# First FFN of a two-layer block: four groups of four and one of six, residual tiles in free space, early first products, weight sums issued one by one

## The chip, the cores and the metric

One core of a Trainium2 chip runs the whole program in one launch. The metric is device microseconds; the time given is the median of the runs, and the kernel before takes 1605.9 us.

## The reference

Two layers work on 512 image tokens and 256 context tokens of 1024 features in float32. Layer 0 mixes by Fourier and long convolution, layer 1 by attention, and each ends in a gated FFN with a three-tap convolution along the tokens. The change lies in the first FFN:

```python
def _conv_ffn(h, w_up, conv_w, conv_b, w_down):        # D_MODEL 1024, D_FF 2816
    gate, val = jnp.split(h @ w_up, 2, axis=-1)
    return (jax.nn.silu(_dwconv3(gate, conv_w, conv_b)) * val) @ w_down

x = x + g2 * _conv_ffn(_modulate(_rms_norm(x, norm2[i]), sh2, sc2), *ffn)
ctx = ctx + cg2 * _conv_ffn(_modulate(_rms_norm(ctx, norm2[i]), csh2, csc2), *ffn)
```

The six shifts, scales and gates of each layer come from `silu(c) @ w_mod + b_mod`; part of that matrix-vector product for layer 1 is done during this FFN.

## The kernel before

Both token sets lie side by side in rows of 772 columns: 512 tokens, two zeros, 256 context tokens, two zeros. Features lie on the 128 partitions, so an activation is eight tiles. A float32 operand is split into a high part (ScalarE, `hi`, L214) and a low rest (VectorE, `lo`, L219), and each product is three matmuls, high by high, high by low and low by high (`mm3`, L239 to L241). A weight is loaded on SyncE's queue (SP) into a `wr` buffer (L227), of which there are three, and split into a `wh` and a `wl` buffer, three each.

The hidden width 2816 is 22 blocks of 128, called f. Blocks 0 and 1 are plain products. For blocks 2 to 21 each 2x2 product of half weights by half activations is done with seven products instead of eight, P1 to P7 (12 matmuls each, 386 columns), from sums of activation quarters (T1 to T4, with halves Th and Tl) and sums of weight quarters (`suma`, `sumb`). A weight sum starts in S1: on GpSimd's queue (POOL) both sums are first filled by a copy, then the second quarter is added by two accumulating transfers. VectorE adds the third quarter in S2 and S4. Ha, La, Hb and Lb split the sums; Rv, Hv, Lv and Rg, Hg, Lg load and split the value and gate quarters.

The elementwise steps of a block: K1, C1 to C4, Ua, Ub and Xv combine the seven products out of PSUM into `fv` and `fg`; Ca, Cb and Cc are the convolution, Si the silu, Ml the product, Ah and Al the split of the result into `acts`.

`UP0_GROUPS` (L164) collects blocks into six groups. For all but the last, Rd, Hd and Ld load and split the blocks of `w_dn`, D multiplies them for each of the eight output tiles m, X scales the result into one of two `delta` tiles (ScalarE, two instructions), and Y adds it to the residual `xs` in DRAM (POOL, accumulating transfer, L1586). For the last group Rk, Hk and Lk prepare all eight weights in tiles of their own (`keep`), the FFN's pools are given up, the residual is loaded from `xs` into tiles `xr` (L1298), and `res_proj` does the closing products: first the 512 image columns for every m, then the 260 others, each added by VectorE to `xr` (L1232). Behind each m the norm of layer 1 takes its sum of squares (L344, L351, L357), scales (L390) and splits.

Rm loads a row block of `wmodT` into a `wr` buffer, 56 in all, and G does one product with it on VectorE (L320, L321), 80 in all: two for each of the first 24 blocks, one for each later one. `self.sb` holds the two vectors for these products.

The order of all these steps is written out in `UP0_ORDER` (L124). Within a `manual_schedule` block every engine executes its own steps in that order, SP and POOL their transfers too; an engine that waits holds back what is behind it. Tiles of a pool wait for the last user of the same memory (`reuse_waits="tile"`). In this stage PSUM has six tiles of 512 columns (`mm`) and two more (`ms`); before the closing products the pool is opened anew with three of 1024.

Of the kernel before, what the change touches and what calls it, by code (L numbers as in the profile page):

```python
# [18 lines left out]
P = 128  # L19
# [105 lines left out]
S1.2 Rv2 Rm0 Rm1 S2.2 T1 G0 U1a T3 Ca0 Hv2 Cb0 Th3 T2 Ha2 Cc0 Th2 T4 Si0 Tl3 Th1.3 U1b Th1.0 Ml0 Th1.1 Th1.2 Tl1.3 Ah0 Tl2 Al0 Lv2 G1 Tl1.0 Tl1.1 Tl1.2  # L125
P1.2 La2 Th4 G2 P2.2 K1.2 Tl4 P5.2 S4.2 Ca1 C1.2 Rv3 G3 Hb2 P6.2 Cb1 Rg2 Rm2 Lb2 Cc1 P7.2 S1.3 Hv3 Ua2 Si1 Lv3 Hg2 Ml1 P1.3 Lg2 Ah1 Xv2 G4 P4.2 K1.3
Al1 Ub2 G5 C2.2 S2.3 P3.2 C4.2 Ha3 S4.3 Ca2 Rv4 La3 P2.3 Hb3 C3.2 Rg3 Cb2 P5.3 Rm3 Lb3 Cc2 S1.4 Hv4 P6.3 C1.3 Si2 Lv4 Hg3 Ml2 P7.3 Lg3 Ah2 Ua3 G6 P1.4
Al2 Xv3 P4.3 G7 K1.4 Ub3 S2.4 C2.3 Ha4 S4.4 P3.3 C4.3 Rm4 La4 Ca3 P2.4 Cb3 Rv5 Hb4 C3.3 Cc3 Rg4 P5.4 Lb4 Si3 G8 S1.5 P6.4 Hv5 Ml3 Hg4 C1.4 Ah3 Lv5 P7.4
Al3 Lg4 P1.5 Ua4 G9 Xv4 P4.4 Rm5 K1.5 Ub4 S2.5 C2.4 Ha5 S4.5 P3.4 C4.4 Rd0.0 La5 Ca4 Rg5 G10 P2.5 Hb5 C3.4 Cb4 P5.5 Hd0.0 G11 Hg5 Cc4 Rm6 P6.5 Lb5 Si4
C1.5 S1.6 Ml4 P7.5 Ld0.0 Ah4 Lg5 Rm7 Al4 D0.0 Ua5 Rd0.1 G12 Xv5 G13 P4.5 Ub5 Rv6 G14 Hd0.1 C2.5 G15 P3.5 Ld0.1 X0.0 Rm8 C4.5 D0.1 S2.6 Ca5 Y0.0 C3.5  # L130
Rd0.2 S4.6 Hv6 Cb5 Ha6 Lv6 Cc5 Rg6 P1.6 X0.1 La6 Si5 G16 Y0.1 P2.6 Hb6 Ml5 K1.6 Hg6 Lb6 Ah5 P5.6 C1.6 Hd0.2 S1.7 Al5 Ld0.2 P6.6 Lg6 G17 P7.6 Ua6 Rd0.3
Xv6 Rm9 D0.2 Ub6 Rd0.4 C2.6 Hd0.3 Ld0.3 G18 Rd0.5 P4.6 X0.2 G19 Y0.2 P3.6 Rv7 C4.6 Ca6 D0.3 Cb6 Hd0.4 Hd0.5 C3.6 Ld0.4 Cc6 Rm10 Ld0.5 Si6 S2.7 Rm11
D0.4 Ml6 X0.3 S4.7 Hv7 Y0.3 G20 Lv7 D0.5 X0.4 G21 Rd0.6 Ha7 Y0.4 G22 Rg7 La7 P1.7 G23 X0.5 Hb7 Rm12 Y0.5 P2.7 Hg7 Lb7 K1.7 Lg7 S1.8 P5.7 Hd0.6 C1.7
Ld0.6 G24 Rd0.7 P6.7 Rv8 G25 P7.7 Rm13 Ua7 Xv7 Hd0.7 D0.6 Ld0.7 Ub7 Rd1.0 C2.7 S2.8 G26 S4.8 P4.7 G27 X0.6 Y0.6 P3.7 C4.7 Ca7 D0.7 Cb7 Hv8 C3.7 Ha8 Cc7
Lv8 Si7 La8 Rg8 P1.8 Rm14 Ah6 Ml7 X0.7 Al6 P2.8 Ah7 Y0.7 K1.8 Al7 Hb8 P5.8 Hg8 G28 Hd1.0 Lb8 P6.8 C1.8 S1.9 Ld1.0 Lg8 Rd1.1 P7.8 G29 Rd1.2 Ua8 Rm15
D1.0 Xv8 Ub8 C2.8 Hd1.1 Ld1.1 Rd1.3 G30 P4.8 X1.0 G31 Y1.0 P3.8 C4.8 Ca8 D1.1 Cb8 Hd1.2 Hd1.3 C3.8 Ld1.2 Cc8 Rd1.4 Ld1.3 Rv9 Si8 Ml8 D1.2 X1.1 Rm16 Ah8
# [24 lines left out]
C2.21 P4.21 X4.3 Y4.3 P3.21 C4.21 Ca21 D4.4 Cb21 Hd4.5 Hd4.6 Ld4.5 C3.21 Rk0 Cc21 Ld4.6 Si21 D4.5 Rk1 X4.4 Ml21 Hd4.7 Y4.4 Ld4.7 Hk0 Rk2 D4.6 Lk0 X4.5
Rk3 Hk1 Y4.5 Lk1 Rk4 D4.7 Hk2 X4.6 Lk2 Rk5 Hk3 Y4.6 Lk3 Ah21 Rk6 X4.7 Al21 Hk4 Y4.7 Lk4 Hk5 Lk5 Rk7 Hk6 Lk6 Hk7 Lk7
"""
UP0_GROUPS = ((0, 4), (4, 8), (8, 12), (12, 15), (15, 18), (18, 22))  # L164


class Builder:
# [94 lines left out]
    def setup(self):  # L262
# [17 lines left out]
        self.sb = self.t(self.sbp, [P, 2, D], F32, "sb")  # L280
# [32 lines left out]
    def gemv_dve(self, i, jt, conds=(0, 1), raw=None):  # L313

        nc = self.nc
        raw = raw or self.wraw(self.I["wmodT"][i, jt])
        for j in conds:
            junk = self.t(self.sbp, [P, D], BF16, "junk", 1)
            acc = self.t(self.sm, [P, 1], F32, "gacc", 4)
            nc.vector.scalar_tensor_tensor(junk, raw, 1.0, self.sb[:, j, :], op0=ALU.mult, op1=ALU.mult, accum_out=acc)  # L320
            nc.vector.tensor_tensor(self.mod[i][:, jt, j : j + 1], acc, self.col(f"bm_{i}", jt), op=ALU.add)  # L321
# [195 lines left out]
    def mixer(self):  # L517
# [26 lines left out]
        with self.tc.manual_schedule(engines={ENG.PE, ENG.DVE, ENG.SP, ENG.Activation}):  # L544
# [102 lines left out]
            for j in range(2):  # L647
                nc.sync.dma_start(self.sb[:, j, :], I["cboth"][j : j + 1, :].partition_broadcast(P))
# [588 lines left out]
    def layer0(self):  # L1237
# [50 lines left out]
        acts, keep = self.ffn_first(hh, hl, u, xs, first, rest.steps, gl1)  # L1288
# [1330 lines left out]
```

## Time and profile before

| | |
|---|---|
| median of 3 runs | 1605.9 us (1604.74 to 1613.03) |
| profiled execution | 1603.81 us, span 1602.0 us |
| TensorE busy | 1534.1 us (96%) |
| VectorE, ScalarE, GpSimd busy | 1304.3, 770.1, 272.9 us |
| read and written in HBM | 200.47 and 24.74 MB |

Times are from one profiled execution, in us from the start of its span. A wait is given with the instruction that ended it. Matmuls overlap: a 386-column matmul is shown as lasting 0.34 us and the next one starts 0.18 us after it, so a product's time is read from starts. "Granted clock" is the share of TensorE's full clock in a stretch.

### The profile page before, as it was taken

The numbers are of one execution on the slowest core, as the hardware profiler recorded it, in microseconds if no ns is written. First come the engines' busy times: TensorE is split into PE (matmuls) and PEld (weight loads), VectorE is DVE, ScalarE is ACT, GpSimd is POOL, SyncE is SP. The second block draws the span as 40 slices with busy tenths as digits, with TensorE's granted clock in tenths as the row PEclk, the third lists the DMA queues.
The fourth block names the chain that finished last, engine by engine and source line by source line (L and its number), as shares of the span: only waits on it lengthen the run. The fifth ranks groups of instructions, "written<-read, shape, count | busy, mean of one in ns | idle before, by whom it ended". The sixth has DMA issues, their size and how long they took to land.

```text
span 1602.0 us, 23289 instructions
## 1 busy us (share of the span) xinstructions
PE 1534.1 (96%) x8728; PEld 1321.0 (82%) x8728; DVE 1304.3 (81%) x2212; ACT 770.1 (48%) x1177; POOL 272.9 (17%) x421
## 2 busy tenths in 40 slices
PE   7999998999899999999899889999999899999998
PEld 5787888888899999999889777666549799999997
DVE  6788869978998769878677576899996899878884
ACT  4451224436444334434344335989874654435442
POOL 0022125201011211212121000222130022112100
PEclk9999998999999999999999999999999999999999
DMA  9336512545368796898974810000025366565543
GB/s 353 115 114 212 170 40 80 191 138 179 94 158 194 182 215 158 211 245 221 245 184 92 279 40 20 7 18 14 1 56 195 92 163 164 152 155 147 147 115 105
DMA packets 87822, 226.73 MB, mean 142 GB/s; under 512 B 10651, under 2 KB 20061, under 8 KB 86685
## 3 DMA queue, kind: packets, MB, share of 16 engines
q1 hardware_dynamic: 62365, 161.18, 30.4%
q0 software_dynamic: 25344, 64.08, 19.7%
q8 instruction: 68, 1.11, 0.3%
q14 instruction: 45, 0.37, 0.1%
HBM read 200.47 MB, written 24.74 MB: 141 GB/s over the span
## 4 chain that ended last, share of the span: by engine, by line
PE 41%; DVE 17%; DMA 8%; issue 3%; ACT 2%; POOL 1%; SPq 0%; DVEq 0%; ACTq 0%; POOLq 0%
PE mm L239 9%; PE mm L241 9%; PE mm L240 9%; DMA wr<-wmodT 4%; DVE junk L320 3%; DVE wl L219 2%; PE pv L1999 2%; PE ms L239 2%; PE ms L240 2%; PE ms L241 2%; DVE S L1975 1%; DMA wr<-w_up 1%; DMA suma<-w_up 1%; PE s L1945 1%; DVE wr L2014 1%
## 5 line engine op out<-in xcount | busy, mean ns | idle before, releaser
L214 ACT ACTIVATE wh<-wr 128x1024 fp32r<-128x1024 f32 (+4 forms) x185 | 157.4, 860 | 234.6 <-PE mm L240 128.4
L239 PE MATMUL mm<-hh,wh 128*128 128x256 f32 (+3 forms) x696 | 231.9, 333 | 4.6 <-ACT wh L214 1.8
L241 PE MATMUL mm<-hh,wl 128*128 128x256 f32 (+3 forms) x696 | 229.2, 329 | 5.9 <-DVE wl L219 5.9
L240 PE MATMUL mm<-hl,wh 128*128 128x256 f32 (+3 forms) x696 | 230.3, 331 | 2.5 <-DVE hl L397 2.3
L219 DVE TENSOR_TENSOR wl<-wr,wh 128x1024 fp32r<-128x1024 f32 (+4 forms) x185 | 182.7, 993 | 27.6 <-ACT wh L214 27.4
L320 DVE SCALAR_TENSOR_TENSOR junk<-wr,sb 128x1024 bf16<-128x1024 f32 x128 | 156.1, 1219 | 22.9 <-DMA wr<-wmodT 22.7
L239 PEld LDWEIGHTS mm<-hh,wh 128*128 128x128 f32 x696 | 133.4, 192 | 17.4 <-ACT wh L214 2.3
L241 PEld LDWEIGHTS mm<-hh,wl 128*128 128x128 f32 x696 | 132.8, 191 | 16.8 <-DVE wl L219 8.6
L240 PEld LDWEIGHTS mm<-hl,wh 128*128 128x128 f32 x696 | 133.2, 191 | 13.2 <-DVE hl L397 3.3
L1999 PE MATMUL pv<-S,V 128*128 128x512 f32 x192 | 93.8, 597 | 2.5 <-ACT S L1978 2.5
L239 PE MATMUL ms<-hh,wh 128*128 128x386 f32 (+2 forms) x240 | 76.7, 319 | 1.9 <-DVE fg L1474 1.2
L241 PE MATMUL ms<-hh,wl 128*128 128x386 f32 (+2 forms) x240 | 76.4, 318 | 1.8 <-DVE wl L219 1.8
L240 PE MATMUL ms<-hl,wh 128*128 128x386 f32 (+2 forms) x240 | 76.2, 318 | 0.0
L1971 POOL PARTITION_ALL_REDUCE mx<-mx x16 | 45.3, 2834 | 163.4 <-DVE mx L1968 163.4
L239 PE MATMUL mm<-ah,wh 128*128 128x512 f32 x176 | 69.6, 396 | 0.0
L240 PE MATMUL mm<-al,wh 128*128 128x512 f32 x176 | 69.6, 396 | 0.0
L241 PE MATMUL mm<-ah,wl 128*128 128x512 f32 x176 | 69.6, 395 | 0.0
L1586 POOL DMA_DIRECT2D xs<-delta x40 | 34.1, 853 | 203.8 <-ACT delta L216 201.3
L1953 ACT ACTIVATE S<-s,rks 128x512 f32<-128x512 f32 x96 | 62.9, 686 | 12.2 <-PE pv L1999 8.3
L239 PE MATMUL mm<-x,wh 128*128 128x512 f32 x192 | 65.3, 340 | 0.0
L240 PE MATMUL mm<-x,wh 128*128 128x512 f32 x192 | 65.2, 339 | 0.0
L241 PE MATMUL mm<-x,wl 128*128 128x512 f32 x192 | 65.0, 338 | 0.0
(503 smaller groups left out, 4521.3 us busy)
## 6 DMA issues: line engine op xcount, KB each, us to landing
wr<-wmodT SPq DMA_DIRECT2D x80, 512.0 KB, 4.6
wr<-w_up SPq DMA_DIRECT2D x48, 512.0 KB, 4.3
sum<-w_up POOLq DMA_DIRECT2D x80, 256.0 KB, 4.3
xs<-delta POOLq DMA_DIRECT2D x40, 386.0 KB, 6.2
wr<-w_dn SPq DMA_DIRECT2D x48, 256.0 KB, 4.1
suma<-w_up POOLq DMA_DIRECT2D x40, 256.0 KB, 5.0
sumb<-w_up POOLq DMA_DIRECT2D x40, 256.0 KB, 5.2
wr<-w_up SPq DMA_DIRECT2D x40, 256.0 KB, 3.5
```

What stands on the lines that cost most here:

```text
L214: self.nc.scalar.activation(dst, src, AF.Copy)
L219: (eng or self.nc.vector).tensor_tensor(dst, src, hi.bitcast(F32), op=ALU.subtract)
L239: mmul(out, wh, xh, start=start, stop=False)
L240: mmul(out, wh, xl, start=False, stop=False)
L241: mmul(out, wl, xh, start=False, stop=stop)
L320: nc.vector.scalar_tensor_tensor(junk, raw, 1.0, self.sb[:, j, :], op0=ALU.mult, op1=ALU.mult, accum_out=acc)
L1586: nc.gpsimd.dma_start(xs[m], k_["x", g, m], accum_op=ALU.add)
L1945: nc.tensor.matmul(ps, k_[0], q[0], start=True, stop=True)
L1953: nc.scalar.activation(c.S[a][j // 3][:, j % 3, :], c.ps[a, j], AF.Copy, scale=c.r[:, g : g + 1])
L1971: nc.gpsimd.partition_all_reduce(c.m[a][:, 1, :], c.m[a][:, 0, :], P, bass.bass_isa.ReduceOp.max)
L1975: v.tensor_tensor(c.S[a][h], c.S[a][h], mb.to_broadcast([P, 3, T]), op=ALU.subtract)
L1999: nc.tensor.matmul(c.P[a], V[:, j, o : o + 128], c.S[a][j // 3][:, j % 3, :], start=j == 0, stop=j == 5)
```

## The change

- The groups are (0, 4), (4, 8), (8, 12), (12, 16) and (16, 22), five instead of six; a D step of the fourth group has four blocks, the closing products have six.
- S1 becomes two steps, Sa and Sb, each a copy and its accumulating transfer on POOL, with a place of its own in the order.
- The two vectors in `sb` become two tiles. From row block 24 on only the first is read, and Rm loads into the place of the second instead of a `wr` buffer.
- `acts` of the slots 4 and 5 move into a pool `hfa` that stays open until attention. The residual tiles are taken from the top down, so that 7, 6 and 5 lie over the FFN's tiles and the first ones in free space.
- Weights 0 and 1 of the closing products are split into the common `wh` and `wl` buffers, 2 to 5 into `keep`, 6 and 7 during the closing products; weight 0 is loaded and split once more for the second pass, whose order is 1, 6, 7, 2, 3, 0, 4, 5.
- Ea does the first five of six blocks of output tiles 0 and 1 (512 columns) before the last block is ready. PSUM keeps its six tiles of 512 columns until the closing products are done.
- `UP0_ORDER` is another order throughout. Its beginning, a later piece and its end are shown.

```diff
 UP0_ORDER = """
-S1.2 Rv2 Rm0 Rm1 S2.2 T1 G0 U1a T3 Ca0 Hv2 Cb0 Th3 T2 Ha2 Cc0 Th2 T4 Si0 Tl3 Th1.3 U1b Th1.0 Ml0 Th1.1 Th1.2 Tl1.3 Ah0 Tl2 Al0 Lv2 G1 Tl1.0 Tl1.1 Tl1.2
-P1.2 La2 Th4 G2 P2.2 K1.2 Tl4 P5.2 S4.2 Ca1 C1.2 Rv3 G3 Hb2 P6.2 Cb1 Rg2 Rm2 Lb2 Cc1 P7.2 S1.3 Hv3 Ua2 Si1 Lv3 Hg2 Ml1 P1.3 Lg2 Ah1 Xv2 G4 P4.2 K1.3
...
-C2.21 P4.21 X4.3 Y4.3 P3.21 C4.21 Ca21 D4.4 Cb21 Hd4.5 Hd4.6 Ld4.5 C3.21 Rk0 Cc21 Ld4.6 Si21 D4.5 Rk1 X4.4 Ml21 Hd4.7 Y4.4 Ld4.7 Hk0 Rk2 D4.6 Lk0 X4.5
-Rk3 Hk1 Y4.5 Lk1 Rk4 D4.7 Hk2 X4.6 Lk2 Rk5 Hk3 Y4.6 Lk3 Ah21 Rk6 X4.7 Al21 Hk4 Y4.7 Lk4 Hk5 Lk5 Rk7 Hk6 Lk6 Hk7 Lk7
+Sa2 Rv2 Sb2 Rv3 Rg2 S2.2 T1 S4.2 T3 U1a Ca0 Hv2 T2 Th3 Cb0 Th2 T4 Ha2 Cc0 Hg2 Tl3 Si0 Th1.3 U1b Ml0 Th1.0 Th1.1 Th1.2 Tl1.3 Ah0 Tl2 Al0 Lv2 Tl1.0 Rm0
+Tl1.1 Tl1.2 La2 Lg2 Sa3 P1.2 Th4 Hb2 P2.2 Tl4 K1.2 Lb2 P5.2 Ca1 C1.2 Hv3 Sb3 Cb1 P6.2 Lv3 Cc1 P7.2 Ua2 Si1 G0 P1.3 Ml1 Xv2 Ah1 S2.3 P4.2 Ub2 K1.3 Al1
...
+P5.16 Si15 Hd3.0 C1.16 Sb17 G64 P6.16 Ml15 Rm41 Ld3.0 Ah15 P7.16 Hv17 Ua16 Rd3.1 Al15 Rg17 Xv16 D3.0 Lv17 Ub16 G65 C2.16 Rm42 S2.17 P4.16 X3.0 S4.17
...
+Lv21 D3.7 Ub20 S2.21 G78 C2.20 Rm55 S4.21 P4.20 Ah18 Rk1 Ah19 Al18 X3.7 P3.20 Al19 Hg21 C4.20 Y3.7 Lg21 Ca20 P1.21 G79 Rk2 Ha21 C3.20 Hb21 Cb20 P2.21
+K1.21 La21 Cc20 P5.21 Hk0 Lb21 Si20 C1.21 P6.21 Ml20 Lk0 Ah20 Rk3 P7.21 Al20 Hk1 Ua21 Lk1 P4.21 Xv21 Rk4 Ub21 C2.21 P3.21 C4.21 Ca21 Ea0 Cb21 Hk2 C3.21
+Hk3 Cc21 Hk4 Lk2 Si21 Lk3 Rk5 Ea1 Ml21 Lk4 Ah21 Al21 Hk5 Lk5
 """
-UP0_GROUPS = ((0, 4), (4, 8), (8, 12), (12, 15), (15, 18), (18, 22))
+UP0_GROUPS = ((0, 4), (4, 8), (8, 12), (12, 16), (16, 22))
...
-        self.sb = self.t(self.sbp, [P, 2, D], F32, "sb")
+        self.sb = [self.t(self.sbp, [P, D], F32, f"sb{j}", 1) for j in range(2)]
...
         self.close("hf2")
-        self.close("psA")
-        self.ps = self.pool("psA", space=PSUM)
-        self.mmw = 1024
         self.zero_pads(hh[:4] + hl[:4])
         self.xp = self.pool("xres")
+        x = [self.t(self.xp, [P, TW], F32, f"xr{d}") for d in reversed(range(KD))][::-1]
         nt = self.pool("nt", bufs=5)
-        x = [self.t(self.xp, [P, TW], F32, f"xr{d}") for d in range(KD)]
         for d in range(KD):
             nc.sync.dma_start(x[d], xs[d])
...
+        def product(m, c, n, first=0, ps=None):
+            ps = ps or self.mm()
+            for k in range(first, nk):
+                w = slice(128 * k, 128 * k + 128)
+                self.mm3(ps[:, 0:n], keep[m][0][:, w], keep[m][1][:, w], acts[k][0][:, c : c + n], acts[k][1][:, c : c + n], k == 0, k == nk - 1)
+            return ps
...
+        for m in range(KD):
+            if keep[m] is None:
+                keep[m] = self.wload(I["w_dn2"][0, m], 128 * nk)
+            add(m, product(m, 0, T, nk - 1, eps[m]) if m in eps else product(m, 0, T), 0, 0, T, 0)
+            ahook(0, m, m)
+        for j, m in enumerate((1, 6, 7, 2, 3, 0, 4, 5)):
+            add(m, product(m, T, 260), T, C0, C0 + C, 1)
+            if j == 0:
+                keep[0] = self.wload(I["w_dn2"][0, 0], 128 * nk)
+            ahook(1, j, m)
...
-        def S1(f):
-            s = k_["sa", f], k_["sb", f] = [one1(tp_[0], 1024, f"sum{q}") for q in "ab"]
-            g, w = I["w_up"][i, f, 0], I["w_up"][i, f, 1]
-            for t_ in s:
-                nc.gpsimd.dma_start(t_[:, 512:1024], g[:, 0:512])
-            for t_, src in zip(s, (g[:, 512:1024], w[:, 0:512])):
-                nc.gpsimd.dma_start(t_[:, 512:1024], src, accum_op=ALU.add)
+        def summed(name, f, other):
+            t_ = k_[name, f] = one1(tp_[0], 1024, name)
+            nc.gpsimd.dma_start(t_[:, 512:1024], I["w_up"][i, f, 0, :, 0:512])
+            nc.gpsimd.dma_start(t_[:, 512:1024], other, accum_op=ALU.add)
...
+        def Ea(m):
+            p_ = eps[m] = self.mm()
+            f0, f1 = UP0_GROUPS[last]
+            for k in range(f1 - f0 - 1):
+                w = slice(128 * k, 128 * k + 128)
+                self.mm3(p_[:, 0:T], keep[m][0][:, w], keep[m][1][:, w], acts[f0 + k][0][:, 0:T], acts[f0 + k][1][:, 0:T], k == 0, False)
...
-            k_["rm", i_, jt] = self.wraw(I["wmodT"][i_, jt])
+            if r < 24:
+                k_["rm", i_, jt] = self.wraw(I["wmodT"][i_, jt])
+            else:
+                k_["rm", i_, jt] = one1(self.sbp, 1024, "sb1")
+                nc.sync.dma_start(k_["rm", i_, jt], I["wmodT"][i_, jt])
```

More of the change, by code (lines that the diff above doesn't have):

```diff
@@ L1287, in layer0 @@
         gl1 += [(1, jt, j) for jt in range(48) for j in ((0, 1) if jt < 16 else (0,))]
-        acts, keep = self.ffn_first(hh, hl, u, xs, first, rest.steps, gl1)
+        acts, keep, eps = self.ffn_first(hh, hl, u, xs, first, rest.steps, gl1)
         self.close("hf2")
-        self.close("psA")
-        self.ps = self.pool("psA", space=PSUM)
-        self.mmw = 1024
         self.zero_pads(hh[:4] + hl[:4])
         self.xp = self.pool("xres")
+        x = [self.t(self.xp, [P, TW], F32, f"xr{d}") for d in reversed(range(KD))][::-1]
         nt = self.pool("nt", bufs=5)
-        x = [self.t(self.xp, [P, TW], F32, f"xr{d}") for d in range(KD)]
         for d in range(KD):
@@ L1306, in ahook, with add @@
                 aw[name] = self.wload(src)
-        sh, sl = [[a[q] for a in acts] for q in range(2)]
-        self.res_proj(0, 5, sh, sl, len(acts), None, x, late, ahook, keep, there=True)
+        nk = len(acts)
+        def product(m, c, n, first=0, ps=None):
[4 more added lines that the diff above has]
+            return ps
+        def add(m, ps, c, a, b, j):
+            nc.vector.scalar_tensor_tensor(x[m][:, a:b], ps[:, a - c : b - c], self.mod[0][:, 40 + m, j : j + 1], x[m][:, a:b], op0=ALU.mult, op1=ALU.add)
+        for m in range(KD):
[8 more added lines that the diff above has]
+            ahook(1, j, m)
+        self.close("psA")
+        self.ps = self.pool("psA", space=PSUM)
+        self.mmw = 1024
         for n in ("kept", "blk0", "xp", "sbp"):
@@ L1529, in Ah @@
             s = f % 6
-            acts[f] = [self.t(xpool, [P, TW], F32R, f"x{2 * s + c}") if s < 4 else one1(hf2(), TW, f"a{s}{c}", F32R) for c in range(2)]
+            acts[f] = [self.t(xpool, [P, TW], F32R, f"x{2 * s + c}") if s < 4 else one1(hf2("a"), TW, f"a{s}{c}", F32R) for c in range(2)]
             self.hi(acts[f][0], k_["q", f])
@@ L1594, in Hk @@
             n = 128 * (UP0_GROUPS[last][1] - UP0_GROUPS[last][0])
-            keep[m] = [one1(kept(), n, f"k{q}{m}", F32R) for q in "hl"]
+            keep[m] = pair(n) if m < 2 else [one1(kept(), n, f"k{q}{m}", F32R) for q in "hl"]
             self.hi(keep[m][0], k_["rk", last, m][:, :n])
@@ L1654, in ffn_first @@
         f0, f1 = UP0_GROUPS[last]
-        return [acts[f] for f in range(f0, f1)], keep
+        return [acts[f] for f in range(f0, f1)], keep, eps
     def attention(self, x, hh, hl, steps, aw):
@@ L1803, in attention @@
             self.close("xres")
+            self.close("hfa")
             self.close("h2p")
```

85 lines of the change are left out of this document (44 added, 41 removed).

## The prediction

> **What bounds the kernel now.** I read the page first, then the waits of TensorE, the stretches of 10 us, and last the chain and the timeline at the places where TensorE stood still.
>
> ```profile
> span 1602.0 us, 23289 instructions
> PE 1534.1 (96%) x8728; PEld 1321.0 (82%) x8728; DVE 1304.3 (81%) x2212; ACT 770.1 (48%) x1177; POOL 272.9 (17%) x421
> ```
>
> TensorE (PE) is busy for 96% of the span, and the change keeps every matmul: the same 22 feature blocks, each multiplied three times over the same columns. So all it can win is TensorE's idle time and the slow matmuls that follow idle time, 68 us in the whole kernel. The first FFN fills roughly 383 to 930 us, and the waits of TensorE from 383 to 960 us are:
>
> ```profile
> PE mm L241 <- DVE wl L219: 7.0, 6, 2.3
> PE mm L239 <- DVE xr L1232: 5.1, 2, 4.9
> PE ms L357 <- DVE nt L351: 4.6, 1, 4.6
> PE mm L239 <- ACT wh L214: 2.2, 3, 1.2
> ```
>
> (us in total, times, longest.) The first and last rows are weights whose low or high half was not split in time; the second is the hand-over from the last feature group to the closing products; the third is the norm behind them. The stretches show where:
>
> ```profile
> 420.00:430.00 10.00, 7.32 (x33) 6.67 (x33) 9.96 (x19) 3.38 (x4) 2.04 (x3) 0.86 0.49 141
> 770.00:780.00 10.00, 7.88 (x44) 6.83 (x44) 7.11 (x12) 5.58 (x9) 1.69 (x2) 1.00 1.00 268
> 790.00:800.00 10.00, 7.68 (x40) 6.92 (x40) 6.70 (x14) 2.00 (x3) 2.23 (x3) 0.96 0.93 223
> 800.00:810.00 10.00, 8.84 (x44) 8.52 (x43) 9.93 (x17) 5.93 (x8) 1.86 (x3) 0.87 0.51 155
> 890.00:900.00 10.00, 5.92 (x26) 4.48 (x24) 3.37 (x5) 2.39 (x4) 0.18 (x1) 0.91 1.03 320
> ```
>
> (PE, weight loads, VectorE, ScalarE, GpSimd, granted clock, DMA share, GB/s.) Three different limits: VectorE full at 420 us, the DMA engines full at 770 to 800 us, and the reload of the residual at 890 us.
>
> **Term A, the hand-over.** The chain of waits, in order of time:
>
> ```profile
> 891.82 7.93 DMA xr<-xs
> 900.03 0.76 DVE xr L1232
> 900.84 0.79 PE mm L239
> ```
>
> The residual tiles may be loaded only when the FFN's own tiles are given up; TensorE fills its three wide PSUM tiles (1024 columns each) and waits for the first residual. The timeline has that pause and the pace before and after it:
>
> ```profile
> 895.29 0.40 PE L240 MATMUL mm<-x,kh 128*128 128x512 f32 x1
> 895.53 0.40 PE L241 MATMUL mm<-x,kl 128*128 128x512 f32 x1
> 900.84 0.79 PE L239 MATMUL mm<-x,kh 128*128 128x512 f32 x1 [4.91 <-DVE xr L1232]
> 905.14 0.39 PE L240 MATMUL mm<-x,kh 128*128 128x512 f32 x1
> ```
>
> The pause is 4.91 us. From 900.84 to 905.14 ten matmuls start, 4.30 us for what takes 10 x 0.24 = 2.4 at the pace of the first two rows: 1.9 more. A is worth 6.8 us. In the changed kernel the loads stand behind Rk5 in SP's queue, which waits for Lk2, some ten steps before the last activation; tiles 0 to 4 lie in free space or over the two delta tiles, and six narrow PSUM tiles take the place of three. The new wait is for the last activation: behind P4.21 TensorE has P3.21 (12 x 0.18 = 2.1) and the two early products (15 x 0.24 = 3.6 each), 9.3 us, and beside them run C4, Ca, Cb, C3, Cc, Si, Ml, Ah and Al with one or two residual splits between, about 9.5 by the rows below. It comes out nearly even: I leave 0.4 us of idle, **A = -6.4**, with -2.4 as the other end (3 us late and a slow stretch again).
>
> **Term B, the start.** Before, four G steps stand ahead of Lb2, which the product P7.2 waits for, and seven ahead of P1.4; after, none and two.
>
> ```profile
> L320 DVE SCALAR_TENSOR_TENSOR junk<-wr,sb 128x1024 bf16<-128x1024 f32 x80 | 97.6, 1221 | 21.2 <-DMA wr<-wmodT 21.2
> L321 DVE TENSOR_TENSOR mod<-gacc,pcol 128x1 f32<-128x1 f32 x80 | 12.8, 160 | 2.8
> L1474 DVE SCALAR_TENSOR_TENSOR fg<-t,mm 128x386 f32<-128x386 f32 x21 | 11.6, 551 | 5.1 <-PE mm L241 5.1
> 423.55 0.44 PE L239 MATMUL mm<-T3h,wh 128*128 128x386 f32 x1 [0.40 <-ACT wh L214]
> 426.45 0.45 PE L241 MATMUL mm<-T3h,wl 128*128 128x386 f32 x1 [2.28 <-DVE wl L219]
> 428.03 0.53 PE L241 MATMUL mm<-T3h,wl 128*128 128x386 f32 x1
> 428.35 0.53 PE L239 MATMUL mm<-T3h,wh 128*128 128x386 f32 x1
> 430.75 0.34 PE L241 MATMUL mm<-hh,wl 128*128 128x386 f32 x1
> 430.93 0.34 PE L239 MATMUL mm<-hh,wh 128*128 128x386 f32 x1
> 435.61 0.45 PE L239 MATMUL mm<-hh,wh 128*128 128x386 f32 x1 [1.33 <-DVE fg L1474]
> ```
>
> A G is 1.22 + 0.16 = 1.4 us of VectorE, so Lb2 comes 5.5 us earlier, more than the 0.40 + 2.28 that P7.2 waited; ten matmuls at 0.32 instead of 0.18 apart cost 1.4 more, and 1.33 waits at 435.61: 5.4 us in all. [...] But VectorE stays full to about 490 us in either order: by P1.6 there are 18 G after and 16 before, so part of the wait returns between blocks 5 and 9. The second sum adds to it: S4.2 now stands right behind T1, while Sb2's two transfers are issued only after Sa2's. I take **B = -2**, ends -5.4 and +2.
>
> **Term C, blocks 14 to 19.** Here the weights land late:
>
> ```profile
> 775.79 0.45 PE L239 MATMUL mm<-hh,wh 128*128 128x386 f32 x1 [1.23 <-ACT wh L214]
> 777.30 0.44 PE L241 MATMUL mm<-hh,wl 128*128 128x386 f32 x1 [0.89 <-DVE wl L219]
> 798.20 0.45 PE L241 MATMUL mm<-hh,wl 128*128 128x386 f32 x1 [1.92 <-DVE wl L219]
> 805.40 0.44 PE L241 MATMUL ms<-hh,wl 128*128 128x386 f32 x1 [1.16 <-DVE wl L219]
> ACT wh L214 <- DMA wr<-w_dn: 63.0, 13, 9.3
> ```
>
> These pauses hold 5.2 us; the stretch at 800 us has 44 matmuls in 8.84 us where 49 fit, 0.9 more; idle behind other causes and the smaller pauses near 720 and 823 us bring it to about 9. The last row (us in total, times, longest, from 383 to 900 us) is the reason: ScalarE stands 63 us before w_dn blocks, and everything behind them in its queue with it. Three wr buffers carry w_up, w_dn and all 56 wmodT rows. The change takes 32 of those rows out (their place is sb1), joins the loads of 128 + 64 KB that blocks 15 to 17 needed, and drops one group. Counted in TensorE work by the two orders, Rd now stands 13 to 19 us ahead of Hd in seven of the eight loads of group 3, before 3 to 12; from block 14 on Rv stands 11 to 15 ahead of Hv, before 3 to 8 but for the last. **C = -7**, ends -9 and 0.
>
> **Term D, the norm.**
>
> ```profile
> 924.86 2.06 DVE nt L390 x3
> 938.10 0.35 DVE nt L351
> 938.49 0.61 PE L357 MATMUL ms<-ones,nt 128*128 128x1 f32 x4 [4.61 <-DVE nt L351]
> ```
>
> VectorE works from 924.86 to 938.45 without rest, and TensorE waits 4.61 us for its last sum. Six blocks instead of four make the second closing pass 8 x 2 x 3 x 0.12 = 5.8 us longer (a 260-column matmul takes half of a 512), which covers it; but the splits of qa0, qa1, kv and the reloaded keep[0] (1.2 us each) now fall into this pass, since W holds residual weights. Two of four inside the chain leave 2 us of idle: **D = -3**, ends -4.6 and 0.
>
> **Term E, the sums.** Sa and Sb now each issue a copy and an add, and POOL waits for the copy to land before the add, with Sb behind Sa.
>
> ```profile
> suma<-w_up POOLq DMA_DIRECT2D x40, 256.0 KB, 5.0
> sumb<-w_up POOLq DMA_DIRECT2D x40, 256.0 KB, 5.2
> L1413 POOL DMA_DIRECT2D sumb<-w_up x20 | 18.0, 902 | 22.6 <-DMA sumb<-w_up 19.5 <-issue 3.1
> POOL suma L1413 <- DMA suma<-w_up: 39.8, 15, 5.8
> ```
>
> From Sa to the landing of Sb's add: 5.0 + 0.9 + 5.2 + 5.2 = 16.3 us. The order leaves three products, one D.0 and P4, 6.4 + 4.3 + 2.1 = 12.8, from Sa17 to S4.17, and as much in blocks 7, 15, 18, 19 and 21. VectorE then stands 3.5 us, with Cb, Xv and the other PSUM readers behind it. From S4 to P7, which reads that sum, TensorE has five products (10.6) and VectorE eight steps of 0.55 to 1.4 us (8): 2.6 us of slack, so 0.9 x 6 = 5 at most reaches TensorE, some hidden by D products. **E = +3**, from 0 to far more (below). [...]
>
> **At nothing:** eight X and Y fewer (ScalarE is busy 48%, GpSimd 17%); fewer and wider splits of w_dn, with as many columns in all; the second load of keep[0], 9 us ahead of its use.
>
> The sum is -6.4 - 2 - 7 - 3 + 3 = -15.4. The profiled execution took 1603.81 us (span 1602.0 and 1.8 around it), 2.1 below the median 1605.9; against the median the forecast is **1590.5**.
>
> **Rivals.** *The sums are late (slower).* The same 16.3 at landings of 6.6 us is 0.9 + 3 x 6.6 = 20.7, 7.9 late, 5.3 after slack, x 6 = 32 us more than E's best case: -18.4 + 32 = +13.6, 1619.5. It decides from E = 26, landings of about 6.3. For it: POOL waited 39.8 us for copies already. Against: the change lowers the traffic that makes landings slow. *Only the edges gain (no change).* The DMA share of 1.00 at 770 us is bandwidth, which the change cuts little, so C = 0, and VectorE's load at the start is only moved, so B = 0: -6.4 - 3 + 3, 1599.5. *The hand-over doesn't do what it says.* If Rk5 waits long, the residual loads queue behind it and A = 0: 1596.9.
>
> **Numbers.** A measurement of this kernel can tell about 0.5%, 8.0 us, from no change. Forecast 0.62, edges only 0.18, hand-over unchanged 0.06, late sums 0.14. The forecast's own range is 1580 to 1600, by the ends of B, C and D; up to 1608 it takes in the edges case with B at its bad end. Left out are late sums and a tail of 0.05 below. Faster: 0.58 of the forecast, half of the hand-over case and little of the edges, 0.62; same 0.24; slower 0.14.
>
> **What would show it.** A: the wait for xr at L1232 gone, pauses under 1 us before the closing products. B: no wait over 1 us at block 2, some between blocks 5 and 9. C: ScalarE's 63 us for w_dn down to a third. D: the wait at L357 under 3 us. E: VectorE waiting for DMA at L1420's line in six blocks. I am wrong if TensorE's waits for wl between 480 and 850 us grow.

## The result and the profile after

The kernel after takes 1596.4 us (median of 20 runs, 1590.3 to 1603.8), the kernel before in the same comparison 1606.0 us: ratio 0.9933, 95% interval 0.9916 to 0.995. That is 9.6 us less. The forecast was 1590.5 us with a range of 1580 to 1608, and 15.4 us less: the sign is right, the size is not, and the profile shows two errors that nearly cancel. The profiled execution took 1596.14 us.

The page of the kernel after, first lines:

```profile
span 1594.4 us, 23204 instructions
PE 1536.5 (96%) x8728; PEld 1325.7 (83%) x8728; DVE 1304.1 (82%) x2205; ACT 762.9 (48%) x1154; POOL 267.1 (17%) x413
```

The waits of TensorE from 383 to 980 us, after (us in total, times, longest), and below them ScalarE's for the last weights, to 900 us:

```profile
PE mm L238 <- DVE nt L389: 5.3, 1, 5.3
PE k L238 <- DVE pt L1762: 3.4, 1, 3.4
PE mm L240 <- DVE wl L218: 3.0, 3, 1.9
PE ms L238 <- DVE fg L1497: 2.0, 2, 1.6
ACT wh L213 <- DMA wr<-w_dn: 10.2, 4, 4.9
```

The wait for `xr` (5.1 us) is gone, `wl` fell from 7.0 to 3.0 us, and ScalarE's wait for `w_dn` from 63.0 to 10.2. But the two longest waits are new, and neither is in the forecast. The stretches, first those of before and then those of after (length, then PE, weight loads, VectorE, ScalarE, GpSimd, granted clock, DMA share, GB/s):

```profile
420.00:500.00 80.00, 75.06 (x408) 71.82 (x407) 79.06 (x132) 33.77 (x43) 15.33 (x21) 0.98 0.64 164
700.00:850.00 150.00, 141.03 (x774) 132.23 (x773) 117.31 (x194) 60.02 (x89) 29.89 (x40) 0.99 0.84 219
870.00:931.00 61.00, 55.85 (x310) 48.74 (x309) 35.34 (x63) 25.45 (x43) 4.44 (x9) 0.94 0.67 200
```

```profile
420.00:500.00 80.00, 74.48 (x402) 70.28 (x402) 77.45 (x133) 32.20 (x42) 14.08 (x19) 0.98 0.62 162
700.00:850.00 150.00, 150.00 (x851) 144.04 (x850) 120.59 (x192) 65.79 (x92) 29.66 (x53) 1.00 0.79 209
848.00:909.00 61.00, 60.96 (x350) 53.91 (x348) 42.51 (x71) 23.70 (x35) 0.19 (x4) 1.00 0.47 167
```

The last row of each is the stretch that ends with the closing products. They end at 931.1 us before and at 909.0 after, 22.1 us earlier: TensorE has 9.0 us less idle time from 700 to 850 us and 5.1 less at the hand-over; the granted clock, 0.99 over 150 us and 0.94 over 61 us, was worth up to 1.5 and 3.7; product P7 of block 2 starts 2.0 earlier, but 1.4 of that is there at the block's first product already, behind steps that the change leaves alone; from 420 to 500 us 0.6 is lost. Together that is up to 20.7 of the 22.1. So the FFN gained some 21 us without that head start, where the terms A, B, C and E promised 12.4.

Then much of it is given back. From the end of the closing products to attention's first value product (`pv<-S,V`) the kernel before needs 86.6 us and the one after 95.9, 9.3 more. These are the rows of before and, below, of after (start, duration, instruction, in brackets the idle time before it):

```profile
930.79 0.28 PE L241 MATMUL mm<-x,kl 128*128 128x260 f32 x1
930.90 0.41 PE L239 MATMUL mm<-hh,wh 128*128 128x512 f32 x1
1017.63 1.10 PE L1999 MATMUL pv<-S,V 128*128 128x512 f32 x2 [0.98 <-ACT S L1978]
```

```profile
908.68 0.28 PE L240 MATMUL mm<-x,kl 128*128 128x260 f32 x1
1004.88 1.10 PE L2035 MATMUL pv<-S,V 128*128 128x512 f32 x2 [0.98 <-ACT S L2014]
```

Here is why, in the timeline of TensorE after:

```profile
914.26 0.77 PE L238 MATMUL mm<-hh,wh 128*128 128x512 f32 x1 [5.30 <-DVE nt L389]
914.83 0.63 PE L239 MATMUL mm<-hl,wh 128*128 128x512 f32 x1
915.26 0.63 PE L240 MATMUL mm<-hh,wl 128*128 128x512 f32 x1
919.52 0.59 PE L356 MATMUL ms<-ones,nt 128*128 128x1 f32 x4
955.06 0.50 PE L238 MATMUL k<-wh,qah 128*128 128x192 f32 x1 [3.44 <-DVE pt L1762]
955.35 0.42 PE L239 MATMUL k<-wl,qah 128*128 128x192 f32 x1
965.91 0.80 PE L238 MATMUL k<-kvh,wh 128*128 128x512 f32 x1
```

Before, the first query products (the first row's kind) ran directly behind the closing products, at 931 us, and TensorE waited behind them for the last sum of the norm. After, TensorE waits 5.30 us ahead of them, and they run at 0.43 us each; the small sums of the norm, ready since about 914.4 us, come only at 919.52. The second wait, 3.44 us ahead of the first key product, did not exist before. Of the 22.1 us, 9.3 go here; 3.6 and 1.5 more in stretches that the change does not touch. The first of these, from the last value product to the first product with `w_dn` in the second FFN, took 135.6 us before, 139.2 after, and between 135.3 and 142.5 in the fourteen kernels of this study, without a pattern. That is scatter, and two profiles alone cannot be compared closer than this.

### The profile page after: what moved, and what is told of

Its sections match the earlier page's. It is cut to its first block, busy times and chain, and to the rows that moved or that the text cites. A ratio compares the mean times of both kernels' runs of the same rounds, so it can differ in the third digit from the quotient of the medians.

```text
span 1594.4 us, 23204 instructions
## 1 busy us (share of the span) xinstructions
PE 1536.5 (96%) x8728; PEld 1325.7 (83%) x8728; DVE 1304.1 (82%) x2205; ACT 762.9 (48%) x1154; POOL 267.1 (17%) x413
## 4 chain that ended last, share of the span: by engine, by line
PE 48%; DVE 17%; DMA 5%; issue 2%; ACT 2%; POOL 1%; DVEq 0%; ACTq 0%; POOLq 0%; SPq 0%
PE mm L238 11%; PE mm L239 11%; PE mm L240 11%; DVE junk L319 3%; DVE wl L218 3%; PE pv L2035 2%; PE ms L240 2%; DMA wr<-w_up 2%; PE ms L238 2%; PE ms L239 2%; DVE S L2011 2%; PE s L1981 1%; DMA wr<-wmodT 1%; DVE wr L2050 1%; DMA sb<-wmodT 1%
## 5 line engine op out<-in xcount | busy, mean ns | idle before, releaser
L213 ACT ACTIVATE wh<-wr 128x1024 fp32r<-128x1024 f32 (+3 forms) x182 | 158.1, 878 | 197.0 <-PE mm L239 135.6
L218 DVE TENSOR_TENSOR wl<-wr,wh 128x1024 fp32r<-128x1024 f32 (+3 forms) x182 | 184.1, 1017 | 22.8 <-ACT wh L213 22.3
L319 DVE SCALAR_TENSOR_TENSOR junk<-wr,sb 128x1024 bf16<-128x1024 f32 x96 | 116.9, 1218 | 7.8 <-DMA wr<-wmodT 7.8
L240 PE MATMUL mm<-x,wl 128*128 128x512 f32 (+1 forms) x224 | 75.8, 338 | 0.8 <-DVE wl L218 0.8
L238 PE MATMUL mm<-x,wh 128*128 128x512 f32 (+1 forms) x224 | 76.1, 340 | 0.0
L239 PE MATMUL mm<-x,wh 128*128 128x512 f32 (+1 forms) x224 | 75.9, 339 | 0.0
L1989 ACT ACTIVATE S<-s,rks 128x512 f32<-128x512 f32 x96 | 62.8, 686 | 12.4 <-PE pv L2035 8.6
L2250 POOL DMA_DIRECT2D sum<-w_up x40 | 23.3, 597 | 244.1 <-DVE wl L218 169.2
```

The lines of the kernel that those rows point to most:

```text
L213: self.nc.scalar.activation(dst, src, AF.Copy)
L218: (eng or self.nc.vector).tensor_tensor(dst, src, hi.bitcast(F32), op=ALU.subtract)
L238: mmul(out, wh, xh, start=start, stop=False)
L239: mmul(out, wh, xl, start=False, stop=False)
L240: mmul(out, wl, xh, start=False, stop=stop)
L319: nc.vector.scalar_tensor_tensor(junk, raw, 1.0, self.sb[j], op0=ALU.mult, op1=ALU.mult, accum_out=acc)
```

## The experiments

Spans and places in us are of the profiled execution, medians and ratios of all runs against the kernel before.

**PSUM banks (e1, e2).** My theory of the two new waits: the wide pool is now opened behind the closing products, and its tiles fall over other banks. By the addresses in the two programs, the query product's tile lay in banks 4-5 before and lies in 0-1 after; bank 1 holds the norm's spread factor, whose last reader is VectorE's scaling (L389). The key/value product's tile lay in 2-3 and lies in 4-5, where the first key product's tile follows it. The rival: these products need the data that the named instructions write.

```diff
-            pqa = self.mm()
+            ppe, pkv, pqa = [self.t(self.ps, [P, 1024], F32, n, 1) for n in ('ppe', 'pkv', 'pqa')]
...
-            pkv = self.mm()
...
-            ppe = self.mm()
```

> After the change, attention's three wide product tiles are placed so that the query product takes banks 4-5, the key/value product 2-3 and the rotary product 0-1, as before the change. Theory (banks): the 5.30 us that TensorE waits ahead of the first query product, and the 3.44 us ahead of the first key product, are waits for a bank (bank 1 with the spread norm factors, banks 4-5 with the key/value product), not for data. Then the query product starts at about 909 us, the first wait is under 1 us, the fold of the context norm comes at about 914.6 us instead of 919.5, the second wait is under 1 us, and the span falls from 1594.4 to 1585-1588 us. Rival (data): the query product needs what VectorE applies last; both waits stay and the span stays at 1593-1596 us.

Median 1585.7 us, ratio 0.9848 (0.9825 to 0.9872), span 1584.2. Its timeline:

```profile
912.82 0.47 PE L238 MATMUL pqa<-hh,wh 128*128 128x512 f32 x1 [1.43 <-DVE xr L1314]
913.13 0.40 PE L239 MATMUL pqa<-hl,wh 128*128 128x512 f32 x1
916.90 0.61 PE L356 MATMUL ms<-ones,nt 128*128 128x1 f32 x4 [1.05 <-DVE nt L350]
948.76 0.34 PE L238 MATMUL k<-wh,qah 128*128 128x192 f32 x1
```

Both waits are gone; 1.43 us remain, for the adds of the last closing products. Not one step moved, only addresses. From the closing products' end (911.4) to the first value product it takes 82.1 us, 13.8 less than after: 8.7 of waits, less the 1.43 and 1.05 that remain, and the rest is pace. The query products are 0.23 us apart here and 0.43 after, and from the first key product to the product `k<-kvh` it takes 6.3 us here and 10.9 after. The theory holds. This version beats both kernels, by 10.7 us against the median of after.

The second wait alone, with the first left in:

```diff
+            k2s = [K2()]
             rt, prot = MS(), [S1(), S1()]
...
-                c.q = K2()
+                c.q = k2s.pop() if k2s else K2()
```

> After the change, with only the first tile of attention's second PSUM pool given out ahead of the small ones, so that the key products take banks 0-1 (the query product's) and not 4-5. Theory (banks): the wait of 3.44 us ahead of the first key product goes, the 5.30 us ahead of the first query product stays; span 1590-1592 us. Rival (data): both stay, 1593-1596 us. Third: the small tiles, now over banks 2, 3 and 5, wait in its place for the rotary and key/value products to be read, and the span stays though the named wait goes.

Ratio 0.9889 (0.9863 to 0.9915), span 1590.7. The wait of 5.30 us is there, that of 3.44 is not, and the small tiles wait for nothing instead; 87.1 us to the first value product. So by these profiles the second wait with its slow pace costs 8.8 us, the first 5.0. The 8.8 is the high end: the five kernels that have both waits at 5.30 and 3.44 us (after, e3, e4, e6, e11) need 95.9, 90.7, 95.9, 90.7 and 93.0 us to the first value product, because the slow pace behind the second lasts longer in some than in others.

**VectorE at the start (term B; e3, e8, e9, e10).** After, the waits of 1.59, 1.91 and 0.45 us lie at 445 to 464 us, beside a VectorE that is busy for 77.45 of 80 us.

```diff
-            self.gemv_dve(i_, jt, (c,), k_["rm", i_, jt])
+            if j < 24:
+                v.tensor_tensor(self.mod[i_][:, jt, c : c + 1], self.col(f"bm_{i_}", jt), self.col(f"bm_{i_}", jt), op=ALU.add)
+            else:
+                self.gemv_dve(i_, jt, (c,), k_["rm", i_, jt])
```

> After the change, with the first 24 of the gate products on VectorE (1.3 us each) left out, an add of 0.16 us in the place of each; the columns that they make are wrong. Theory (VectorE bounds blocks 2 to 5): the 5.5 us that TensorE is idle between 440 and 500 us shrink to under 1 us, the closing products end 5-6 us earlier than 908.9 us, span 1588-1590 us. Rival (late weights): the idle time there stays over 4 us and the closing products end within 1.5 us of 908.9.

The stretch of its start:

```profile
420.00:500.00 80.00, 79.28 (x446) 76.64 (x445) 60.57 (x105) 33.70 (x44) 15.53 (x21) 1.00 0.73 193
```

Idle time is 0.7 us instead of 5.5, the clock 1.00, and the closing products end at 901.2 us, 7.8 earlier than after and more than the 5 to 6 expected (4.8 of idle time, up to 1.6 of clock, and 1.4 elsewhere, inside the scatter). Ratio 0.9851 (0.9822 to 0.988). This alone does not rule out late weights, for rows that nothing reads free their ring buffers sooner too (DMA share 0.73 instead of 0.62). The trace of after does: from 437 us until past both longer waits VectorE goes from step to step without waiting for a load, and the wait of 1.91 us ends with the last of these steps, the low half of block 5's value weights. So B's cause is VectorE's work. Two tries to use that, both on the kernel of e1. First, to do this work later: the Rm and G steps of `UP0_ORDER` are spread evenly from block 4's P1 to their old end.

> The kernel of e1_banks with the gate rows' loads and products moved later in the written order, the first from block 3 to block 4 and the rest stretched evenly up to the old end; nothing is left out. Theory (VectorE bounds blocks 2 to 5, and has room after 500 us): TensorE's idle time between 440 and 500 us falls from about 6 us to under 2, closing products end at 903-906 us, span 1576-1580 us. Rival (loads that move later make the weights of later blocks late): the gain at 440-500 us is given back between 600 and 850 us, span 1583-1587 us.

Median 1613.0 us, ratio 1.0041 (1.0024 to 1.0058): slower than before the change. From 440 to 460 us it has 0.4 us of idle time instead of e1's 3.5, as wanted, and then it loses 6.8 us from 460 to 500, 6.3 from 500 to 600, and in the stretch

```profile
700.00:850.00 150.00, 142.89 (x801) 134.18 (x800) 113.92 (x182) 60.27 (x87) 28.43 (x37) 1.00 0.78 204
```

with ScalarE's wait for `w_dn` back at 32.8 us, from 12.0 in e1. The rival is right in kind, though the span of 1608.5 us is far beyond its 1583 to 1587: moving these steps moves loads, and other weights become late. Second, to give work to GpSimd without moving a load, the sums of blocks 3 to 6 in S2 and S4:

```diff
-            v.tensor_tensor(s[:, 0:512], s[:, 512:1024], k_["rv", f][:, 0:512], op=ALU.add)
+            e = nc.gpsimd if 3 <= f <= 6 else v
+            e.tensor_tensor(s[:, 0:512], s[:, 512:1024], k_["rv", f][:, 0:512], op=ALU.add)
```

> The kernel of e1_banks with the two 512-wide weight-sum adds of blocks 3 to 6 (0.69 us each on VectorE) done on GpSimd, which has 1.5 to 2.3 us of work in each 10 us there; loads and order stay. Theory (VectorE bounds blocks 2 to 5): VectorE loses 5.5 us of work, TensorE's idle time between 440 and 500 us falls from 6.3 us to 2-4, closing products end at 906-909 us instead of 911.0, span 1580-1582 us. Rival (the sums then come too late, since GpSimd adds them slower and behind its own waits for the copies): idle time there stays or grows, span 1584-1590 us.

Median 1592.4 us, ratio 0.991 (0.9897 to 0.9923), 6.7 slower than e1; 9.5 us idle from 420 to 500. Besides the late sums that the rival names there is a cause that I had not in mind, as GpSimd's timeline and VectorE's at the same time show:

```profile
443.25 1.60 POOL L1441 TENSOR_TENSOR sa<-sa,wr 128x512 f32<-128x512 f32 x1
444.94 1.63 POOL L1445 TENSOR_TENSOR sb<-sa,wr 128x512 f32<-128x512 f32 x1
```

```profile
443.62 1.80 DVE L218 TENSOR_TENSOR wgl<-wr,wgh 128x512 fp32r<-128x512 f32 x1
445.34 2.31 DVE L319 SCALAR_TENSOR_TENSOR junk<-wr,sb 128x1024 bf16<-128x1024 f32 x1
448.24 1.22 DVE L319 SCALAR_TENSOR_TENSOR junk<-wr,sb 128x1024 bf16<-128x1024 f32 x1
```

VectorE's steps are lengthened by 1.12 and 1.09 us while GpSimd adds, 2.2 for a pair that would have cost VectorE 1.38. Beside all four pairs its steps are lengthened by about 7.4 us, an estimate from their durations here and in e1. That gives VectorE some 2 us more to do, not 5.5 less. The same with the low halves of the gate weights of these blocks on GpSimd as well:

> The kernel of e9 with the low halves of the 512-wide gate weights of blocks 3 to 6 (0.68 us each on VectorE) done on GpSimd too. Theory: VectorE loses 8.2 us of work in all, idle time between 440 and 500 us falls to under 2 us, closing products end at 904-907 us, span 1578-1581 us. Rival (GpSimd, in order behind its waits, hands the low halves out late): idle time grows by 2 us or more, span 1585-1592 us.

Median 1600.3 us, ratio 0.9967 (0.9953 to 0.998), closing products to 929.4 us: worse again, 14.5 us over e1, and idle time from 440 to 500 us grows from 8.5 to 10.8 us, as the rival said.

**The hand-over (term A; e4, e6, e5).** First the place of the residual tiles alone:

```diff
-        x = [self.t(self.xp, [P, TW], F32, f"xr{d}") for d in reversed(range(KD))][::-1]
         nt = self.pool("nt", bufs=5)
+        x = [self.t(self.xp, [P, TW], F32, f"xr{d}") for d in range(KD)]
```

> After the change, with the residual tiles given out after the norm's temporaries and in forward order, as before the change, so that they lie over space that the FFN still uses; first products stay split and PSUM tiles stay 512 wide. Theory (free space did it): a wait of 4-5 us comes back at the hand-over to the closing products, which end at 912-914 us instead of 908.9. Rival (six narrow PSUM tiles instead of three wide ones, and the split products, cover it anyway): the residual tiles land later, but TensorE waits under 1 us more, and the closing products end within 1 us of 908.9.

Ratio 0.9902 (0.9874 to 0.993). No wait at the hand-over. The closing products end at 911.7, but what is late is late at 490 us already: from the last product with T3 to the last closing product it takes 57.5 us in both kernels. The rival is right. With Ea0 and Ea1 taken out of the order as well:

> After the change without the split first products and with the residual tiles given out late and forward; the six narrow PSUM tiles stay. Theory (the split products cover the last activation's lead): 1.5-5 us of wait come back at about 860 us, closing products end at 913-916 us. Rival (narrow tiles cover it: six products can run before the first residual tile is needed): under 1 us of wait beyond that, closing products end within 1 us of 911.3. The waits of 5.3 and 3.4 us ahead of attention stay in both.

Ratio 0.9922 (0.9894 to 0.9949), closing products to 909.8 us, 57.6 us from the last product with T3, no wait: rival again. Then everything at the hand-over as before the change, also the wide PSUM tiles (and so the old banks):

```diff
         self.close("hf2")
+        self.close("psA")
+        self.ps = self.pool("psA", space=PSUM)
+        self.mmw = 1024
...
-        self.close("psA")
-        self.ps = self.pool("psA", space=PSUM)
-        self.mmw = 1024
```

> After the change with the whole hand-over as before it: PSUM opened anew with wide tiles ahead of the closing products, no split first products, residual tiles given out late and forward; groups, order, sums and places stay new. Theory A (the hand-over's parts together are worth 6-7 us): a wait of 4-6 us comes back near 865-870 us and the closing products end at 915-918 us instead of 909-911. Rival (the new order alone brings the last activation early enough): under 2 us of wait there, end at 910-913 us. Either way the query product's tile no longer lies over the norm's: both waits of 5.30 and 3.44 us are gone, and from the closing products' end to the first value product it takes 84-88 us, not 96.

Ratio 0.9887 (0.986 to 0.9914). TensorE waits 0.99 us at the hand-over, not 4 to 6 (for VectorE's reading of the last block's products in PSUM, not for a residual tile), and from the last product with T3 it takes 58.7 us, 1.2 more. The end at 915.3 falls into the theory's numbers, but for another reason (3.0 us of idle time between 600 and 700). Both waits ahead of attention are gone, with 85.1 us to the first value product, as both expectations said.

**Late weights (term C; e12, e7).** Is it the gate rows in the ring? In the kernel before, they are taken away from the 25th on, and their products left in place:

```diff
-            k_["rm", i_, jt] = self.wraw(I["wmodT"][i_, jt])
+            k_["rm", i_, jt] = self.wraw(I["wmodT"][i_, jt]) if r < 24 else self.sb[:, 0, :]
```

> Before the change, with the gate rows from the 25th on not loaded; their products stay on VectorE, at the same places, but read the first conditioning vector in place of the row, so their columns are wrong. It takes 32 loads of 512 KB and their places in the ring of weight tiles away and leaves order, groups and sums alone. Theory C as predicted (these loads make the FFN's weights late in blocks 14 to 19): ScalarE's wait for the last weights falls from 63.0 us to under 20, and the closing products end 7-10 us earlier than 930.9. Rival (the written order gives those weights too little lead whatever shares the ring): both move by under 2 us. Between: the loads are a part of it, 2-6 us.

```profile
700.00:850.00 150.00, 150.00 (x851) 144.58 (x851) 123.93 (x205) 65.50 (x96) 31.52 (x42) 1.00 0.64 139
ACT wh L214 <- DMA wr<-w_dn: 27.0, 5, 6.3
```

The 9 us of idle time are gone, with the old order, groups and sums, and the closing products end at 920.1 us, 11.0 earlier. Ratio 0.9924 (0.9899 to 0.9949). ScalarE's wait falls less than expected. So it is these loads. The run takes their traffic away too (139 GB/s instead of 219), but traffic alone is not what held the weights: the kernel after moves 209 GB/s in this stretch, at a DMA share of 0.79, and has no idle time. Do they only need another place, then? In the kernel before, with `sb` in two tiles and

```diff
-            k_["rm", i_, jt] = self.wraw(I["wmodT"][i_, jt])
+            if r < 24:
+                k_["rm", i_, jt] = self.wraw(I["wmodT"][i_, jt])
+            else:
+                k_["rm", i_, jt] = one1(self.sbp, 1024, "sb1")
+                nc.sync.dma_start(k_["rm", i_, jt], I["wmodT"][i_, jt])
```

> Before the change, with one part of it: from the 25th gate row on, rows are loaded into the place of the second conditioning vector and no longer into the ring of weight tiles. Order, groups and sums stay as before. Theory C (late weights in blocks 14 to 19 come from the gate rows in the ring): ScalarE's wait for the last weights of the FFN, 63.0 us in 13 times, falls to a third, the closing products end 5-7 us earlier than 930.9, ratio 0.996. Rival (the order made them late): wait and end move by under 2 us, ratio 1.000.

Median 1642.7 us, ratio 1.0223 (1.0198 to 1.0248): neither, it is 35 us slower. ScalarE waits longer for `w_dn`, and SP's queue, which issues the loads, shows why:

```profile
ACT wh L214 <- DMA wr<-w_dn: 85.4, 13, 11.7
SPq L1610 <- DMA sb<-wmodT: 112.4, 31, 6.1
SPq L1610 <- DVE mod L321: 59.3, 28, 6.4
```

One place for all rows means that each row's load waits in SP's queue for the row before it to land and be used, with the weights behind it. After the change SP waits for the same two things, 85.8 and 59.3 us, but it has no idle time from 700 to 850 us. That its order issues the weights far enough ahead fits this and was not measured by itself. Without the new order the place does harm. The new order with the rows left in the ring was not tried: as written, its steps would wait for each other.

**The sums in series (term E; e11).** The second accumulating transfer is left out:

```diff
-            nc.gpsimd.dma_start(t_[:, 512:1024], other, accum_op=ALU.add)
+            if name == "sa":
+                nc.gpsimd.dma_start(t_[:, 512:1024], other, accum_op=ALU.add)
```

> After the change, with the second accumulating add of each block (the one into the second sum tile) left out; that sum is incomplete. The prediction's term E (the adds in series make VectorE late in six blocks): the closing products end about 3 us earlier. Corrected reading of the code (VectorE's second add reads the first sum and the value weights, not the accumulated half, and only ScalarE's copy waits for it, 9.2 us in 6 times, off the path): closing products within 1.5 us of 909-911 us, span within 2 us of 1592-1595.

Closing products to 910.2 us, with the 909.0 to 911.7 of the five kernels that share the FFN of after or differ from it only at the hand-over's place and split; ratio 0.989 (0.9878 to 0.9903), span 1589.6, a little under what either reading expected of it; all that it gains on after's 1594.4 lies behind the FFN. The corrected reading fits: no wait of TensorE in the FFN after leads back to these adds. The end alone could not tell the 3 us of the forecast from nothing: counted from block 2's first product, e11 takes 494.6 us to the end of the closing products, and the five take 495.6 to 500.2.

## Why the prediction was right and wrong

- **A, forecast -6.4: about right in size (5.1 us of idle time and up to 3.7 of clock are gone), wrong in its working.** I gave it to the free space and the early products; e4 and e6 show that neither matters. e5 shows that the new order and groups alone leave about 1.2 us, which six narrow tiles then remove. Two things in them can do it, and they were not separated: a closing product has six blocks, 18 x 0.24 = 4.3 us, so that three wide tiles last 12.9 us instead of 8.6; and the last `delta` transfer is issued 23 us before the first residual load, not 2, as the rows of before (first two) and of e5 show (times are of the first and the last one):

```profile
L1586 POOL DMA_DIRECT2D xs<-delta x10: 838/852/867, 781.3 to 889.3; - x10
L1298 SPq DMA_DIRECT2D xr<-xs x8: 319/397/550, 891.3 to 897.9; - x8
```

```profile
L1609 POOL DMA_DIRECT2D xs<-delta x6: 843/864/1211, 781.0 to 844.7; - x6
L1297 SPq DMA_DIRECT2D xr<-xs x8: 319/456/1317, 867.7 to 872.5; - x8
```

- **B, -2: right for the start, but nothing was gained over the stretch.** From block 2's first product to the end of its P7 it takes 10.6 us instead of 14.8, about the 4.1 us of waits and slow pace that I had counted there. Waits come back at once: 1.59 us at block 3's P3, sooner than the blocks 5 to 9 that I named, and 1.91 at block 5's P1. Idle time from 420 to 500 us is 5.5 us instead of 4.9. That VectorE bounds it is shown by its timeline and by e3.
- **C, -7: right cause, too small.** I ended the range at -9, the idle time; with the clock it was about 10.5 by the traces, and e12 gives 11.0 for the loads alone. "Down to a third" for the 63 us was passed, at 10.2. What I had not seen is that the new place alone would be harmful (e7).
- **D, -3: the step that failed.** The longer second pass does cover the norm, as e1 shows: 82.1 us instead of before's 86.6 to the first value product, 4.5 less, at the good end of my range. But the term counted only data and engines. It gave no price to the line that opens the wide PSUM pool behind the closing products, and with the banks so given it measured +9.3 (+4.1 to +9.4 in the five kernels with these banks), against a bound of 0 on the bad side. The wait at L357 that I expected under 3 us was indeed gone; a longer one stood in front of it.
- **E, +3: not found.** I named the wrong waiter: S4 on VectorE reads the first sum and the value weights, not the half that Sb's transfers fill. Only ScalarE's Hb waits for that half, 9.2 us in six times, off the path. The rival "late sums" goes with it.

So the likeliest case had the right sign by mechanisms that mostly held, and that its number came near is luck: C was larger and E absent, together about 7 us, while D was 12.3 worse, and 5.1 us more went in stretches that I had not counted. "Only the edges gain" was wrong about C, and the hand-over did change. What stays open: how much of C each of order and place gives, since neither can stand alone, which part of the hand-over's change brings A, and the scatter in the FFN's end among kernels with the same steps there, 2.7 us (4.6 counted from block 2's first product).

## What to carry to other kernels

When a pool of PSUM is closed and opened at another point, look up which banks its first tiles now take, and who reads these banks last: here a tile's address made waits of 5.30 and 3.44 us where no data passes, and giving the tiles out in another order (e1) repaired it, at no cost. Compare such a change at milestones on the bounding engine (end of the stage, first product of the next) and not by the span alone, because a gain of 22 us and a loss of 9 lay side by side here. And a load that gets a place of its own no longer takes a ring buffer, but it can still hold back what is behind it in its queue: in e7 SP waited 112.4 us for such rows to land and 59.3 for their use, and ScalarE's wait for `w_dn` grew from 63.0 to 85.4 us.

## What was not expected of the hardware

- The slow pace behind a pause can cost as much as the pause: that of 3.44 us and the pace behind it cost up to 8.8 us, by the profiles of after and e2. After the pauses of 5.30 and 3.44 us the matmuls run at 0.43 instead of 0.23 us (512 columns) and 0.21 instead of 0.11 (192 columns), in the second case for some 15 us; the granted clock is 0.53 from 914 to 920 us and 0.50 from 955 to 970. The length of a pause alone does not tell the pace behind it: behind e1's pause of 1.43 us it stays at 0.23, but behind e1's pause of 0.46 us ahead of `k<-kvh` it is 0.43 for 3.4 us, and at the start before, behind pauses of 0.40 and 2.28 us, it is 0.32 instead of 0.18 (386 columns) from 427.1 to 430.3 us.
- How long the slow pace lasts is not fixed by the pause. Behind the same pause of 3.44 us the same steps from the first key product to the first value product took 45.8 us in e3 and e6, 47.4 in e11 and 49.8 in after and e4; the nine kernels without that pause took 43.2 to 45.7.
- The granted clock was lower where two short pauses lay close together than where there was one. Ahead of the FFN's first products five kernels (before, e6, e8, e11, e12) have pauses of 0.8 to 1.3 us twice within 3.2 us, and their granted clock from 374 to 392 us is 0.91 (before: 0.83 and 1.17 us). The other nine have one pause of 1.16 or 1.17 us there, and it is 1.00.
- VectorE's steps took longer beside GpSimd's adds. In e9 a VectorE step with two inputs took 1.80 us, instead of 0.68 in e1, beside an add of 1.60 on GpSimd, and the next one 2.31 instead of 1.22 beside an add of 1.63. So the cost of handing a pair over, 2.2 us, exceeded the work, 1.38.
